# Output pairs of a two-layer encoder: one weight sum moved from an accumulating DMA to VectorE, and residual and memory loads spread over the last pair

## The chip, the cores and the metric

The kernel runs on one core of one Trainium2 chip. The metric is device time in microseconds (us). Before the change it is 1529.16 us, the median of three runs (1528.39 to 1529.31). TensorE is called PE in the profile, VectorE DVE, ScalarE ACT, GpSimd POOL and SyncE SP.

## The reference

An encoder of two layers over 512 positions of width 2048, in float32. Of one layer (cut):

```python
h = rmsnorm(x, pre_norm_g[l])
z = h @ w_in[l]                    # 2048 x 4928, split into latents, conv, memory query, gate
a_out = mla_attention(q, k, v)     # 8 heads, 512 positions
c_out = short_gated_conv(gb, gc, xin, conv_w[l])
m_out = memory_attention(q_mem, rmsnorm(mem, mem_norm_g[l]), w_mk[l], w_mv[l])
y = jnp.concatenate([a_out, c_out, m_out], axis=-1) * jax.nn.silu(gate)
o = y @ w_o[l]                     # 2048 x 2048
x = x + rmsnorm(o, post_norm_g[l])
```

The change is about the last two lines: the output projection, and the residual sum behind its norm.

## The kernel before, in words

**Products in two halves.** Every float32 operand is split into a high half (fp32r) and the rest, and each product is three matmuls (`mm3`, lines 245, 246, 247: high by high, high by low, low by high). `prep` splits a weight block of 128x1024: ScalarE casts the block `wr` into `wh` (line 172), VectorE subtracts to get `wl` (line 173). For the memory's weights a gain is multiplied in, in two halves of 512 columns (lines 177 and 178).

**Seven products for eight.** A projection is computed by pairs of 512 output columns in the Strassen-Winograd form: the weight's four blocks B11, B12, B21, B22 and four sums of them, the left operand's blocks and sums, and seven products P1 to P7. One product is four steps (c = 0 to 3), each with one weight block of 128x1024, 512 KB. `unit` says where a step's weight operand comes from. In the output pairs P1 uses B11, loaded by SP into a tile T, which has a buffer of its own for each c. P5 uses T after B12 was added to it (this sum is T1), P6 after B22 was added, P4 after B21 was added. P2 uses B21 by itself, P3 uses B22, and P7 uses B22 after B12 was added. Each of these additions is an **accumulating DMA** that POOL issues (`more`, line 134, `accum_op=ALU.add`): it is issued as soon as both halves of the block's previous use are split. So one output pair has 16 of them: four each for P5, P6, P4 and P7.

**The order of the work.** The output projection of a layer has two pairs, g0 (the first) and g1 (the last). Each goes through the passes P2, P1, P5, P6 and P3 in turn, P7, P4; P2 of g0, and of g1, is put elsewhere. `Program.run` walks over the steps. Before each it has SP load weight blocks (`load`, a ring of RAW = 8 buffers, in which T keeps its own while it is in use) and prepares (`prep`) blocks two steps ahead. Evictions, gains and norms are put off (`defer`) and taken from a list as each step's `room` allows. PE, SP and POOL run in the order in which the program is written; the order on DVE and ACT is set by a scheduler at build time. The order also fixes each queue: an engine waits for its next instruction's operands even where a later one could run.

**Behind the last pair.** `fetch(t)` is a DMA on POOL that loads 128 rows of the residual x (or, in layer 1, of the scratch `xs`), 1 MB, into a tile `xr` (line 1125). `mem_reload(h)` loads one half of the turned memory, two tiles mH and mL of 1 MB each, from the scratch `mTd`, on POOL (line 671). When a row tile's four column blocks are done, `factor` reduces its squares (`tot`, DVE, line 1148), POOL computes the factor r (`ms` line 255, `r` line 257), and DVE adds the scaled output to xr in two halves (line 1155); POOL writes the new rows to `xs` (line 1159), or SP the output in layer 1. Products are evicted on DVE by lines 430, 457 and 460 and on ACT by line 465; line 1110 squares and line 1115 multiplies by the gain on DVE. In layer 1 P4 of the last pair holds its four weight blocks at once in tiles T4h and T4l (`hold`). The memory's products (mk, mv) of the next layer start right behind P4 of layer 0, with the mH and mL of `mem_reload(0)`.

Of the kernel before, what the change touches and what calls it, by code (L numbers as in the profile page):

```python
# [5 lines left out]
F32 = mybir.dt.float32  # L6
# [3 lines left out]
ALU = mybir.AluOpType  # L10
AX = mybir.AxisListType

P = 128
# [3 lines left out]
NT = S // P  # L17
# [46 lines left out]
class Unit:  # L64
# [2 lines left out]

    def __init__(self, key, loads=(), more=None, alloc=None, gain=None):  # L70
        self.key = key
        self.loads = loads
        self.more = more
        self.alloc = alloc
        self.gain = gain


class Program:
# [19 lines left out]
    def add(self, fn, units=(), room=0.0, ahead=None):  # L98

        self.steps.append((list(units), fn, room, self.ahead if ahead is None else ahead))  # L100
# [14 lines left out]
    def run(self):  # L115
        nc = self.nc
        raw, hip, lop = self.pools
        seq = [u for us, *_ in self.steps for u in us]
        tiles, outs = {}, {}
        at = {"load": 0, "prep": 0}  # L120
        users = {}
        for c, u in enumerate(seq):
            users.setdefault(u.key, []).append(c)
        after = {a: b for cs in users.values() for a, b in zip(cs, cs[1:])}
        first_more = [c for c, u in enumerate(seq) if u.more is not None and users[u.key][0] == c]

        def move(engine, t, off, src, **kw):
            n = 1
            for d in src.shape[1:]:
                n *= d  # L130
            dst = t[:, off:off + n]
            if len(src.shape) == 3:
                dst = dst.rearrange("p (a b) -> p a b", b=src.shape[2])
            engine.dma_start(dst, src, **kw)  # L134
            return off + n

        def load(upto):
            upto = max(upto, self.early)
            while at["load"] < min(upto, len(seq)):
                u = seq[at["load"]]  # L140
                if u.loads:
                    t = raw.tile([P, 1024], F32, tag="raw", name=f"wr{len(tiles)}")
                    off = 0
                    for src in u.loads:
                        off = move(nc.sync, t, off, src)
                    tiles[u.key] = t[:, :off]
                at["load"] += 1

        def more(c):
            u = seq[c]  # L150
            move(nc.gpsimd, tiles[u.key], 0, u.more, accum_op=ALU.add)

        self.load = load

        def prep(upto):
            while at["prep"] < min(upto, len(seq)):
                c = at["prep"]
                load(c + 1)
                while first_more and first_more[0] <= c + self.more_ahead:
                    load(first_more[0] + 1)  # L160
                    more(first_more.pop(0))
                u = seq[c]
                src = tiles[u.key]
                at["prep"] += 1
                n = src.shape[-1]
                if u.alloc is None:
                    hi = hip.tile([P, 1024], F32R, tag="wh", name=f"wh{c}")
                    lo = lop.tile([P, 1024], F32R, tag="wl", name=f"wl{c}")
                else:
                    hi, lo = u.alloc()  # L170
                if u.gain is None:
                    nc.scalar.copy(hi[:, :n], src)  # L172
                    nc.vector.tensor_tensor(lo[:, :n], src, hi[:, :n].bitcast(F32), op=ALU.subtract)  # L173
                else:
                    for k, g in enumerate(u.gain()):
                        h = slice(k * (n // 2), (k + 1) * (n // 2))
                        nc.scalar.activation(hi[:, h], src[:, h], AF.Copy, scale=g)  # L177
                        nc.vector.scalar_tensor_tensor(lo[:, h], src[:, h], g, hi[:, h].bitcast(F32),  # L178
                                                       op0=ALU.mult, op1=ALU.subtract)
                outs[c] = (hi[:, :n], lo[:, :n])  # L180
                if c in after:
                    more(after[c])

        self.prep = prep
        c = 0
        spare = 0.0
        for units, fn, room, ahead in self.steps:
            n = len(units)
            if n:
                load(c + n + self.ahead + self.loads_ahead)  # L190
                prep(c + n + ahead)
            fn(*[outs.pop(c + i) for i in range(n)])
            c += n
            spare = min(spare + room, 2.5)
            while self.queue and spare >= self.queue[0][0]:
                cost, put_off = self.queue.pop(0)
                spare -= cost
                put_off()


def encoder(tc, x, mem, positions, pre_norm_g, w_in, q_norm_g, w_uq, kv_norm_g, w_ukv, conv_w,
# [3 lines left out]
    nc = tc.nc  # L205
# [18 lines left out]
    G = {}  # L224
# [180 lines left out]
    STEADY = [["P1"], ["P5", "P2"], ["P6", "P3"], ["P7"], ["P4"]]  # L405
    SECOND = [["P2"], ["P1"], ["P5"], ["P6", "P3"], ["P7"], ["P4"]]

    def group(left, key, w, block, slot, passes, final, hold=None, by_two=False):

# [5 lines left out]

        def unit(q, c):
            def of(name, *loads, more=None, alloc=None):
                return Unit((key, name, c), [block(h, j, c) for h, j in loads],  # L420
                            None if more is None else block(*more, c), alloc)
            if q == "P1":
                return of("P1" if apart else "T", (0, 0))
            if q == "P5":
                return of("T", *([(0, 0)] if apart else []), more=(0, 1))
            return {"P6": lambda: of("T", more=(1, 1)), "P4": lambda: of("T", more=(1, 0), alloc=hold),
                    "P2": lambda: of("P2", (1, 0)), "P3": lambda: of("B22", (1, 1)),
                    "P7": lambda: of("B22", more=(0, 1))}[q]()
# [84 lines left out]

        def room(q, c):
            if c < 3:
                return 1.4
            moves = {"P1": passes is SECOND, "P2": passes is not SECOND, "P5": apart, "P7": 1 + apart}
            return 1.4 - 1.4 * moves.get(q, 1)

# [555 lines left out]
    def out_proj(l):  # L1075
# [17 lines left out]
        def block(g):  # L1093
            def f(h, j, c):
                r = h * 1024 + c * 256
                k = (2 * g + j) * 512
                return w_o[l, r:r + 256, k:k + 512].rearrange("(a p) c -> p a c", p=P)
            return f

        def slot(g):  # L1100
            return lambda i, j, tt: og(2 * i + tt)[:, (2 * g + j) * 512:(2 * g + j + 1) * 512]
# [32 lines left out]
            hold_n[0] += 1  # L1134
            return tuple(t[:, k * 1024:(k + 1) * 1024] for t in st["hold"])

        g0 = group(G["left"], ("o", l, 0), 512, block(0), slot(0), SECOND, fin(0))
        g1 = group(G["left"], ("o", l, 1), 512, block(1), slot(1), SECOND, fin(1), hold if last else None)
        return g0, g1, gains, fetch

    def residual(l, st, t):
# [40 lines left out]
    def put(*passes):  # L1182
        for steps in passes:
            for s in steps:
                add(*s)
# [26 lines left out]
    for l in range(depth):  # L1212
# [7 lines left out]
        if l == 0:  # L1220
            add(use)
            def turn_half(t, h, on=None):
                return lambda: transpose_rows(0, t, G[f"hs{t}"], (2 * h, 2 * h + 1), on)
            add(turn_half(0, 0))
            add(lambda: first_rows(1, (0,)))
            add(pr.begin_prep(1))
            add(lambda: left_half(0, (0,)))
            add(pr.begin_prep(2))
            add(turn_half(1, 0, nc.scalar))
            add(lambda: first_rows(1, (1,)))  # L1230
            add(lambda: left_half(1, (0,)))
            add(pr.begin_prep(3))
            add(lambda: first_factor(2))
            add(turn_half(0, 1))
        else:
            ms = mem_steps(l)
            put(ms[:1])
            add(use)
            for n in range(16):
                t, q = n // 4, n % 4  # L1240
                if q == 0:
                    add(lambda t=t: pr.until(lambda: f"hs{t}" in G))
                add(lambda t=t, q=q: transpose_rows(l, t, G[f"hs{t}"], (q,)))
                if t < 2 and q % 2:
                    add(lambda t=t, q=q: left_half(t, (q // 2,)))
                if t >= 2 and q == 3:
                    add(lambda t=t: right_half(t - 2))
                put(ms[n + 1:n + 2])
        (a, b), (a1, b1) = gs[0][:2], gs[1][:2]
        add(owns[0])  # L1250
        if l == 0:
# [77 lines left out]
                G["src"], G["dst"] = x[0], dram.tile([S, D], F32, name="xs")  # L1329
        add(route)  # L1330
        add(gains(1))
        put(*g1[1:3])
        put(g1[3])
        for t in range(NT):
            add(fetch(t))
        if l + 1 < depth:
            add(lambda: mem_reload(0))
        put(g1[4])
        if l + 1 < depth:
            add(lambda: mem_reload(1))  # L1340
        put(g1[5])
        if l + 1 == depth:
            add(pr.settle)

# [26 lines left out]
```

## Time and profile before

| what | value |
|---|---|
| median of three runs | 1529.16 us |
| profiled execution, its own time | 1529.26 us |
| span of the profiled execution | 1527.5 us |
| granted TensorE clock, mean | 0.994 |
| PE busy | 1493.4 us (98%) |
| DVE busy | 1040.1 us (68%) |
| DMA of POOL's queue | 141.57 MB, 48.5% of 16 engines' span |
| DMA of SP's queue | 132.68 MB, 26.7% of 16 engines' span |

A row of a timeline reads: start in us, time in us, engine, line, operation, output and inputs, count, and in brackets the idle time of the engine just before and what ended it. A row of the chain of work reads: start, time, what held the end at that moment. In layer 0 the last pair's P5 runs from 705.6 us, P6 and P3 from 716.5, P7 from 738.4, P4 from 749.1; in layer 1 the same stages come some 750 us later.

### The profile page before, as it was taken

Reading aid. Unit: us, or ns where it says so; the run is one execution under the profiler, and the core shown is the slowest. Engines: PE = TensorE matmul, PEld = TensorE weight load, DVE = VectorE, ACT = ScalarE, POOL = GpSimd, SP = SyncE. Lnnn points to the kernel's source line nnn. Section 1 sums busy time; section 2 is a strip of 40 time slices with the busy share of each in tenths; the row PEclk is TensorE's granted clock in tenths of the full one; section 3 lists DMA queues with packets and bytes.
Section 4 is the critical chain, followed back from the end, with each engine's and each line's share of the span. In section 5 each row is a group of like instructions: output and inputs, shape, how many; then the busy total and the mean of one; then the engine's idle time right before and its main releaser. Section 6 shows DMA issues by size and latency. Waiting matters only on the chain.

```text
span 1527.5 us, 20239 instructions
## 1 busy us (share of the span) xinstructions
PE 1493.4 (98%) x7613; PEld 1281.3 (84%) x7613; DVE 1040.1 (68%) x1398; ACT 864.7 (57%) x1335; POOL 314.9 (21%) x313
## 2 busy tenths in 40 slices
PE   9999999999999999999999999999999999999996
PEld 7888888988898888888788888888988888888884
DVE  6965675565968668865778766675566586687656
ACT  7733534454768768645578434434454686775542
POOL 1233131332000000324320333131332000003231
PEclk9999999999999999999999999999999999999998
DMA  8999898989581112699997999897989411048895
GB/s 330 216 213 224 204 174 174 199 196 256 164 264 56 42 42 82 109 202 197 313 332 239 238 224 226 187 176 168 198 207 222 130 59 39 29 111 146 203 200 222
DMA packets 146934, 275.59 MB, mean 180 GB/s; under 512 B 17340, under 2 KB 40212, under 8 KB 143508
## 3 DMA queue, kind: packets, MB, share of 16 engines
q0 software_dynamic: 65600, 141.57, 48.5%
q1 hardware_dynamic: 81104, 132.68, 26.7%
q8 instruction: 59, 0.97, 0.3%
q14 instruction: 39, 0.32, 0.1%
q10 hardware_dynamic: 132, 0.05, 0.0%
HBM read 259.59 MB, written 14.68 MB: 180 GB/s over the span
## 4 chain that ended last, share of the span: by engine, by line
PE 85%; DVE 4%; DMA 3%; issue 3%; ACT 3%; POOL 2%; POOLq 0%; DVEq 0%; ACTq 0%
PE P L246 20%; PE P L247 20%; PE P L245 19%; PE ptp L973 2%; PE tps L731 1%; DMA mL<-mTd 1%; PE o L246 1%; PE sc L245 1%; PE mk L246 1%; PE sc L246 1%; PE sc L247 1%; PE mk L247 1%; PE o L247 1%; PE o L245 1%; DVE wl L173 1%
## 5 line engine op out<-in xcount | busy, mean ns | idle before, releaser
L173 DVE TENSOR_TENSOR wl<-wr,wh 128x1024 fp32r<-128x1024 f32 (+1 forms) x408 | 486.4, 1196 | 334.6 <-ACT wh L172 332.2
L172 ACT CAST wh<-wr 128x1024 fp32r<-128x1024 f32 (+1 forms) x408 | 420.6, 1033 | 482.5 <-PE P L247 418.2
L246 PE MATMUL P<-wl,S 128*128 128x512 f32 (+1 forms) x896 | 344.2, 384 | 2.8 <-DVE wl L173 2.8
L245 PE MATMUL P<-wh,S 128*128 128x512 f32 (+1 forms) x896 | 346.0, 386 | 0.0
L247 PE MATMUL P<-wh,S 128*128 128x512 f32 (+1 forms) x896 | 343.4, 383 | 0.0
L134 POOL DMA_DIRECT2D wr<-in_w_in_dram x160 | 193.4, 1209 | 484.5 <-DVE wl L173 365.2
L246 PE MATMUL P<-wl,A 128*128 128x512 f32 (+1 forms) x656 | 251.9, 384 | 2.1 <-DVE wl L173 2.1
L245 PE MATMUL P<-wh,A 128*128 128x512 f32 (+1 forms) x656 | 253.1, 386 | 0.2 <-ACT wh L172 0.2
L247 PE MATMUL P<-wh,A 128*128 128x512 f32 (+1 forms) x656 | 251.6, 384 | 0.5 <-DVE A L251 0.5
L246 PEld LDWEIGHTS P<-wl,S 128*128 128x128 f32 x896 | 168.3, 188 | 33.7 <-DVE wl L173 4.4
L247 PEld LDWEIGHTS P<-wh,S 128*128 128x128 f32 x896 | 168.2, 188 | 30.4
L245 PEld LDWEIGHTS P<-wh,S 128*128 128x128 f32 x896 | 168.1, 188 | 29.6 <-ACT wh L172 0.2
L134 POOL DMA_DIRECT2D wr<-in_w_o_dram x64 | 77.3, 1208 | 505.0 <-DVE rec L961 352.0
L246 PEld LDWEIGHTS P<-wl,A 128*128 128x128 f32 x656 | 123.2, 188 | 24.4 <-DVE wl L173 2.9
L247 PEld LDWEIGHTS P<-wh,A 128*128 128x128 f32 x656 | 123.1, 188 | 23.3 <-DVE A L251 1.2
L245 PEld LDWEIGHTS P<-wh,A 128*128 128x128 f32 x656 | 123.1, 188 | 22.3 <-ACT wh L172 0.6
L959 ACT ACTIVATE P<-sc,nm 128x512 f32<-128x512 f32 (+1 forms) x96 | 59.9, 624 | 36.4 <-DVE nm L956 35.8
L962 ACT ACTIVATE P<-P,rec 128x512 f32<-128x512 f32 (+1 forms) x96 | 62.1, 658 | 5.0 <-DVE rec L961 5.0
L956 DVE TENSOR_REDUCE nm<-sc 128x1 f32<-128x512 f32 (+1 forms) x96 | 57.2, 596 | 10.0 <-PE sc L954 6.3
L251 DVE TENSOR_TENSOR PT<-ptp,PT 128x512 fp32r<-128x512 f32 (+1 forms) x96 | 56.5, 594 | 8.5 <-ACT PT L250 8.1
L178 DVE SCALAR_TENSOR_TENSOR wl<-wr,cols,wh 128x512 fp32r<-128x512 f32 x64 | 46.2, 747 | 18.2 <-ACT wh L177 18.0
L177 ACT ACTIVATE wh<-wr,cols 128x512 fp32r<-128x512 f32 x64 | 44.2, 722 | 25.2 <-PE mk L246 10.9
(267 smaller groups left out, 2182.4 us busy)
## 6 DMA issues: line engine op xcount, KB each, us to landing
wr<-in_w_in_dram POOLq DMA_DIRECT2D x128, 512.0 KB, 6.9
wr<-in_w_in_dram SPq DMA_DIRECT2D x112, 512.0 KB, 5.6
wr<-in_w_o_dram POOLq DMA_DIRECT2D x64, 512.0 KB, 7.3
wr<-in_w_o_dram SPq DMA_DIRECT2D x48, 512.0 KB, 3.9
wr<-in_w_in_dram POOLq DMA_DIRECT2D x32, 416.0 KB, 5.4
wr<-in_w_in_dram SPq DMA_DIRECT2D x24, 416.0 KB, 4.3
wr<-in_w_mk_dram SPq DMA_DIRECT2D x16, 512.0 KB, 6.9
wr<-in_w_mv_dram SPq DMA_DIRECT2D x16, 512.0 KB, 4.5
```

The costliest lines, as they stand in the source:

```text
L134: engine.dma_start(dst, src, **kw)
L172: nc.scalar.copy(hi[:, :n], src)
L173: nc.vector.tensor_tensor(lo[:, :n], src, hi[:, :n].bitcast(F32), op=ALU.subtract)
L177: nc.scalar.activation(hi[:, h], src[:, h], AF.Copy, scale=g)
L178: nc.vector.scalar_tensor_tensor(lo[:, h], src[:, h], g, hi[:, h].bitcast(F32), op0=ALU.mult, op1=ALU.subtract)
L245: nc.tensor.matmul(ps, ah, bh, start=first, stop=False, **kw)
L246: nc.tensor.matmul(ps, ah, bl, start=False, stop=False, **kw)
L247: nc.tensor.matmul(ps, al, bh, start=False, stop=last, **kw)
L251: nc.vector.tensor_tensor(lo, src, hi.bitcast(F32), op=ALU.subtract)
L956: nc.vector.tensor_reduce(nmax, ps, axis=AX.X, op=ALU.max, negate=True)
L959: nc.scalar.activation(pt, ps, AF.Exp, bias=nmax, accum_out=tot)
L962: nc.scalar.activation(pt, pt, AF.Copy, scale=rec)
```

## The change

Two things are changed. First, in both output pairs T1 is summed by VectorE: B12 is loaded by SP into a raw buffer of its own (`plus`), and `prep` adds it to T ahead of P5's split. The accumulating DMA of P5 is not issued, and the room of P5's first three steps goes from 1.4 to 0.2. The other accumulations (P6, P4, P7) stay. Second, the four residual loads and the memory's reloads are issued at other steps of the last pair.

```diff
                     for src in u.loads:
                         off = move(nc.sync, t, off, src)
                     tiles[u.key] = t[:, :off]
+                if u.plus is not None:
+                    t = raw.tile([P, 1024], F32, tag="raw", name=f"wr{len(tiles)}")
+                    off = move(nc.sync, t, 0, u.plus)
+                    tiles[at["load"]] = t[:, :off]
                 at["load"] += 1
...
                 src = tiles[u.key]
+                if u.plus is not None:
+                    nc.vector.tensor_tensor(src, src, tiles[c], op=ALU.add)
...
-                if c in after:
+                if c in after and seq[after[c]].more is not None:
                     more(after[c])
...
+                loads = [block(h, j, c) for h, j in loads]
+                more = None if more is None else block(*more, c)
+                if q in by_vector:
+                    return Unit((key, name, c), loads, plus=more, alloc=alloc)
+                return Unit((key, name, c), loads, more, alloc=alloc)
...
             if c < 3:
-                return 1.4
+                return 0.2 if q in by_vector else 1.4
...
-        g0 = group(G["left"], ("o", l, 0), 512, block(0), slot(0), SECOND, fin(0))
-        g1 = group(G["left"], ("o", l, 1), 512, block(1), slot(1), SECOND, fin(1), hold if last else None)
+        g0 = group(G["left"], ("o", l, 0), 512, block(0), slot(0), SECOND, fin(0), by_vector=("P5",))
+        g1 = group(G["left"], ("o", l, 1), 512, block(1), slot(1), SECOND, fin(1), hold if last else None,
+                   by_vector=("P5",))
...
                 put(ms[n + 1:n + 2])
+                if n == 0:
+                    add(lambda: mem_reload(1))
...
-        put(*g1[1:3])
-        put(g1[3])
-        for t in range(NT):
-            add(fetch(t))
+        put(g1[1], g1[2][:1])
+        add(fetch(0))
+        put(g1[2][1:], g1[3][:1])
+        add(fetch(1))
+        put(g1[3][1:4])
+        add(fetch(2))
+        put(g1[3][4:])
         if l + 1 < depth:
             add(lambda: mem_reload(0))
-        put(g1[4])
-        if l + 1 < depth:
-            add(lambda: mem_reload(1))
-        put(g1[5])
+        put(g1[4][:2])
+        add(fetch(3))
+        put(g1[4][2:], g1[5])
```

PE's order of matmuls is the same. POOL's queue in layer 0, at the end of the last pair, before (`wr<-in_w_o_dram` is an accumulating DMA of 512 KB, `xr` a residual load of 1 MB, `mH` and `mL` the memory):

```order
L134 DMA wr_6208<-in_w_o_dram 128x2x512
L134 DMA wr_6446<-in_w_o_dram 128x2x512
L255 TENSOR_SCALAR ms_6613<-tot_637_6611 128x1
L257 TENSOR_TENSOR r_6615<-ms_6613,mhalf 128x1
L1125 DMA xr_6617<-in_x_dram 128x2048
L1125 DMA xr_6619<-in_x_dram 128x2048
L1125 DMA xr_6621<-in_x_dram 128x2048
L1125 DMA xr_6623<-in_x_dram 128x2048
L671 DMA mH_6625<-mTd 128x2048
L671 DMA mL_6626<-mTd 128x2048
L1159 DMA xs<-xr_6617 128x1024 x2
```

And now, from the second residual load on:

```order
L1136 DMA xr_6502<-in_x_dram 128x2048
L135 DMA wr_6379<-in_w_o_dram 128x2x512
L135 DMA wr_6198<-in_w_o_dram 128x2x512
L135 DMA wr_6427<-in_w_o_dram 128x2x512
L1136 DMA xr_6557<-in_x_dram 128x2048
L135 DMA wr_6216<-in_w_o_dram 128x2x512
L135 DMA wr_6464<-in_w_o_dram 128x2x512
L262 TENSOR_SCALAR ms_6635<-tot_640_6633 128x1
L264 TENSOR_TENSOR r_6637<-ms_6635,mhalf 128x1
L682 DMA mH_6639<-mTd 128x2048
L682 DMA mL_6640<-mTd 128x2048
L1171 DMA xs<-xr_6425 128x1024 x2
```

Three residual loads (the first stands three accumulations ahead of these rows' start) are now among the accumulations, the last of which, wr_6464, is the sum of B22 for P7's last step; mH and mL stand right behind the first r. The fourth residual load stands behind the second r, the second memory reload behind the third pair of writes to xs.

VectorE in the second pair, at P1 and P5 in layer 0, where the additions are; before (wr_5484 and wr_5539 are P4's blocks of the first pair, wr_6152 and the following ones T of the second):

```order
L173 TENSOR_TENSOR wl_6235<-wr_5484,wh_6234 128x1024
L1115 TENSOR_TENSOR og_5553<-og_5553,g_616_5834 128x512
L1115 TENSOR_TENSOR og_5564<-og_5564,g_616_5834 128x512
L173 TENSOR_TENSOR wl_6251<-wr_5539,wh_6250 128x1024
L173 TENSOR_TENSOR wl_6267<-wr_6152,wh_6266 128x1024
L173 TENSOR_TENSOR wl_6284<-wr_6172,wh_6283 128x1024
L430 TENSOR_TENSOR og_5553<-og_5553,P_617_5841 128x512
L430 TENSOR_TENSOR og_5564<-og_5564,P_618_5842 128x512
L173 TENSOR_TENSOR wl_6312<-wr_6190,wh_6311 128x1024
```

And now:

```order
L180 TENSOR_TENSOR wl_6263<-wr_5539,wh_6262 128x1024
L180 TENSOR_TENSOR wl_6281<-wr_6160,wh_6280 128x1024
L170 TENSOR_TENSOR wr_6160<-wr_6160,wr_6242 128x1024
L180 TENSOR_TENSOR wl_6299<-wr_6180,wh_6298 128x1024
L441 TENSOR_TENSOR og_5553<-og_5553,P_617_5846 128x512
L441 TENSOR_TENSOR og_5564<-og_5564,P_618_5847 128x512
L170 TENSOR_TENSOR wr_6180<-wr_6180,wr_6260 128x1024
L1126 TENSOR_TENSOR og_5553<-og_5553,g_615_5838 128x512
L1126 TENSOR_TENSOR og_5564<-og_5564,g_615_5838 128x512
L180 TENSOR_TENSOR wl_6326<-wr_6198,wh_6325 128x1024
```

Line 170 is the new addition; it stands behind the split of P1's block of the same T. In the first pair three of its four stand among the last attention work, ahead of the stage that starts at 639 us.

VectorE in layer 1, from P7's last split on, before:

```order
L1148 TENSOR_REDUCE tot_1260_13084<-ssqo_1191_12026 128x1
L1148 TENSOR_REDUCE tot_1271_13142<-ssqo_1195_12037 128x1
L173 TENSOR_TENSOR wl_13119<-wr_12919,wh_13118 128x1024
L1155 SCALAR_TENSOR_TENSOR xr_13090<-og_12025,r_13088,xr_13090 128x1024 x2
L460 SCALAR_TENSOR_TENSOR og_12027<-P_1267_13102,og_12027 128x512
L460 SCALAR_TENSOR_TENSOR og_12038<-P_1268_13103,og_12038 128x512
L1115 TENSOR_TENSOR og_12027<-og_12027,g_1253_12782 128x512
L173 TENSOR_TENSOR T4l_13123<-wr_12626,T4h_13122 128x1024
L173 TENSOR_TENSOR T4l_13123<-wr_12646,T4h_13122 128x1024
```

And now (T4l of the first two blocks stands in one row each, the second of them eleven rows above these, ahead of P3's last split):

```order
L1160 TENSOR_REDUCE tot_1263_13122<-ssqo_1191_12042 128x1
L1160 TENSOR_REDUCE tot_1270_13172<-ssqo_1195_12053 128x1
L1167 SCALAR_TENSOR_TENSOR xr_12914<-og_12041,r_13126,xr_12914 128x1024
L180 TENSOR_TENSOR wl_13149<-wr_12953,wh_13148 128x1024
L1167 SCALAR_TENSOR_TENSOR xr_12914<-og_12041,r_13126,xr_12914 128x1024
L180 TENSOR_TENSOR T4l_13181<-wr_12688,T4h_13180 128x1024
L1167 SCALAR_TENSOR_TENSOR xr_12991<-og_12052,r_13176,xr_12991 128x1024 x2
```

The T4 splits of the first two blocks moved ahead of the residual; one half of the residual now stands ahead of P7's last split (wl_13149), in layer 0 as in layer 1.

More of the change, by code (lines that the diff above doesn't have):

```diff
@@ L64, with __init__ @@
 class Unit:
-    def __init__(self, key, loads=(), more=None, alloc=None, gain=None):
+    def __init__(self, key, loads=(), more=None, plus=None, alloc=None, gain=None):
         self.key = key
@@ L73, in __init__ @@
         self.more = more
+        self.plus = plus
         self.alloc = alloc
@@ L406, in encoder, with group @@
     SECOND = [["P2"], ["P1"], ["P5"], ["P6", "P3"], ["P7"], ["P4"]]
-    def group(left, key, w, block, slot, passes, final, hold=None, by_two=False):
+    def group(left, key, w, block, slot, passes, final, hold=None, by_two=False, by_vector=()):
         bk = {}
@@ L419, in of @@
             def of(name, *loads, more=None, alloc=None):
-                return Unit((key, name, c), [block(h, j, c) for h, j in loads],
-                            None if more is None else block(*more, c), alloc)
+                loads = [block(h, j, c) for h, j in loads]
[3 more added lines that the diff above has]
+                return Unit((key, name, c), loads, more, alloc=alloc)
             if q == "P1":
```

## The prediction

> **What bounds the kernel now.** I read the page first, then the list of waits of TensorE, then the chain of work and the timelines around the three longest waits.
>
> ```profile
> span 1527.5 us, 20239 instructions
> PE 1493.4 (98%) x7613; PEld 1281.3 (84%) x7613; DVE 1040.1 (68%) x1398; ACT 864.7 (57%) x1335; POOL 314.9 (21%) x313
> PE P L246 <- DVE wl L173: 5.0, 5, 1.4
> PE P L245 <- ACT T4h L172: 4.7, 1, 4.7
> PE mk L246 <- DMA mL<-mTd: 3.2, 1, 3.2
> PE mk L247 <- DVE wl L178: 1.3, 1, 1.3
> ```
>
> TensorE is busy 98% of the span, so only two things can be won: its waits, and the time in which it runs at a lower rate behind a wait. The list of waits has the columns waiting engine and line, releaser, total us, times, longest. Three of its rows belong to this change: the 4.7 on T4h, the 3.2 on mL and parts of the first. Here is how the one on mL arises, at the end of layer 0.
>
> ```profile
> 742.36 1.47 POOL r L257
> 743.82 2.71 DMA xr<-in_x_dram
> 746.53 19.35 DMA mL<-mTd
> 749.88 2.48 DVE L1155 SCALAR_TENSOR_TENSOR xr<-og,r,xr 128x1024 f32<-128x1024 f32 x2 [3.72 <-DMA xr<-in_x_dram]
> 751.81 0.39 PE L245 MATMUL P<-wh,A 128*128 128x512 f32 x1
> 753.55 0.50 PE L246 MATMUL P<-wl,A 128*128 128x512 f32 x1 [1.36 <-DVE wl L173]
> 762.34 0.36 PE L245 MATMUL mk<-mH,wh 128*128 128x256 f32 x1 [0.54 <-DMA mH<-mTd]
> 766.50 0.21 PE mk L247
> 770.98 0.21 PE mk L247
> 784.06 0.12 PE mk L245
> ```
>
> POOL starts the four residual loads only behind r, at 743.82, and the memory loads behind them. VectorE waits 3.72 for the first residual load, with the splits of P4 queued behind it, so TensorE waits 1.36 at 753.55. mL takes 19.35 from its issue at 746.53, to 765.88, because six transfers of 1 MB lie in a row: TensorE waits 0.54 and then 3.2. After that its matmuls start 0.21 apart for 24 of them (766 to 771), where at 784 the same matmul takes 0.12: 24 x 0.09 = 2.2 more. This place costs 0.54 + 3.2 + 2.2 = **5.9**, and the one on VectorE **1.36**.
>
> The end of layer 1 is the other place:
>
> ```profile
> 1492.88 5.13 DMA xr<-xs
> 1498.12 2.48 DVE xr L1155 x2
> 1502.92 0.95 ACT T4h L172
> 1503.91 0.80 PE L245 MATMUL P<-T4h,A 128*128 128x512 f32 x1 [4.71 <-ACT T4h L172]
> 1505.17 0.80 PE L246 MATMUL P<-T4l,A 128*128 128x512 f32 x1 [0.46 <-DVE T4l L173]
> 1506.19 0.63 PE L245 MATMUL P<-T4h,A 128*128 128x512 f32 x1
> 1508.75 0.43 PE L245 MATMUL P<-T4h,A 128*128 128x512 f32 x1
> 1509.02 0.40 PE L246 MATMUL P<-T4l,A 128*128 128x512 f32 x1
> 681.66 0.23 PE P L247
> ```
>
> The residual load is issued at 1492.88, VectorE stands until 1498.12, and what is queued behind it (the eviction of P7, then the squares and T4h on ScalarE) ends in a wait of 4.71. Between 1503.91 and 1509.02 TensorE starts ten matmuls in 5.11; at its usual 0.23 apart (as at 681.66) they take 2.3. So this place costs 4.71 + 2.8 = **7.5**. The Trainium skill ("TensorE: Matmul & The Clock Gate", Part 1: The HAM clock gate) says that an idle window of about 3.4 us drops the clock to a half until some 3.4 us of work have gone by; the trace agrees: spacing 0.43 behind the wait of 4.71, 0.21 against 0.12 behind one of 3.2, and nothing of the kind behind 1.36.
>
> A smaller place lies in the first pair of layer 0:
>
> ```profile
> 669.04 9.69 DMA wr<-in_w_o_dram
> 681.16 0.50 PE L246 MATMUL P<-wl,S 128*128 128x512 f32 x1 [0.76 <-DVE wl L173]
> ```
>
> An accumulating DMA lands 9.69 after its issue, since others lie ahead of it: **0.76**.
>
> **The change part by part.** *The sum by VectorE.* It takes 16 accumulating DMAs off POOL's queue (4 for each of 2 pairs in 2 layers) and adds 16 plain loads by SP and 16 additions of 128x1024.
>
> ```profile
> L173 DVE TENSOR_TENSOR wl<-wr,wh 128x1024 fp32r<-128x1024 f32 (+1 forms) x408 | 486.4, 1196 | 334.6 <-ACT wh L172 332.2
> 639.20:650.00 10.80, 10.80 (x49) 8.96 (x48) 10.80 (x12) 8.08 (x11) 5.83 (x5) 1.00 0.94 159
> 705.50:716.40 10.90, 10.90 (x50) 9.03 (x49) 7.16 (x8) 6.15 (x9) 4.77 (x4) 1.00 1.13 207
> 749.10:761.80 12.70, 11.34 (x49) 8.73 (x47) 11.44 (x14) 8.77 (x14) 3.72 (x6) 1.00 1.03 417
> ```
>
> The L173 row is the same kind of instruction on the same shape at 1.196, so the additions are 16 x 1.2 = 19.1 of VectorE's time. In the second pair VectorE is busy 7.16 of 10.9 in the stage of P5 (the columns of the windows are PE, PEld, DVE, ACT, POOL, clock, DMA share, GB/s), so four additions of 4.8 come to 12.0 for that stage and its neighbours; the evictions, which the plan puts off while P5 runs (room 0.2 for 1.4), go to later stages. In the first pair the stage from 639.2 is full (10.80 of 10.80), but by VectorE's order three of the four additions stand before it. Nothing uncovered is the one bound, one addition of 1.2 in each layer the other; nearest are the half-idle stages, so I take 0.3 in all (0 to 2.4). SP's 16 loads come before each pair's queue on POOL is busy; I take 0 for them and keep their price for a rival.
>
> *What goes.* The wait at 681.16 (0.76): the four accumulations ahead of it are gone. The 1.36 at 753.55, the 5.9 at mL (both residual data and memory are now asked for earlier; mH and mL stand directly behind r), the 7.5 at T4h (the first two T4 splits are now ahead of the residual). Of the 1.3 on the memory's split, mk L247 (queued behind a residual that waits for r) I take half, 0.7, since that wait for r stays (0 to 1.3). Sum: 0.76 + 1.36 + 5.9 + 7.5 + 0.7 = **16.2**.
>
> *What comes.* Three residual loads of 1 MB now lie in POOL's queue among the second pair's 12 accumulations, ahead of the last two, and TensorE needs the last one, the sum of B22 for P7's last step.
>
> ```profile
> 701.41 1.23 DVE L173 TENSOR_TENSOR wl<-wr,wh 128x1024 fp32r<-128x1024 f32 x1 [1.50 <-ACT wh L172]
> 704.13 1.23 DVE L173 TENSOR_TENSOR wl<-wr,wh 128x1024 fp32r<-128x1024 f32 x1 [1.50 <-ACT wh L172]
> 707.06 1.19 POOL L134 DMA_DIRECT2D wr<-in_w_o_dram  x1 [2.83 <-DMA wr<-in_w_o_dram]
> 720.11 1.21 POOL L134 DMA_DIRECT2D wr<-in_w_o_dram  x1 [1.14 <-DVE wl L173]
> 730.28 1.21 POOL L134 DMA_DIRECT2D wr<-in_w_o_dram  x1 [1.35 <-DVE wl L173]
> 732.97 1.21 POOL L134 DMA_DIRECT2D wr<-in_w_o_dram  x1 [1.47 <-DVE wl L173]
> wr<-in_w_o_dram POOLq DMA_DIRECT2D x64, 512.0 KB, 7.3
> 1491.49 1.05 ACT L172 CAST wh<-wr 128x1024 fp32r<-128x1024 f32 x1 [0.69 <-DMA wr<-in_w_o_dram]
> ```
>
> When due: a step takes 2.72 (701.41 to 704.13). P4's second step starts at 751.81, so P7's last starts two steps earlier, at 746.4, and 0.23 later needs the low half of its split, behind 1.05 on ScalarE and 1.23 on VectorE: the sum must land by 744.2 (with 0.1 for hand-offs). In layer 1 P7 ends 4.71 before 1503.91, at 1499.2; its last step starts at 1496.5 and the sum is due at 1494.2. When it lands: before, at 732.97 + 7.3 = 740.3 in layer 0 and at 1491.45 in layer 1. The queue serves one accumulation in (730.28 - 720.11) / 4 = 2.54. One residual load costs it between 2.5 (1 MB at the 417 GB/s of the stage from 749.1) and 5.1 (1492.88, alone); I take 2.9, near the lower end, since the 5.1 holds a latency that is hidden in a queue. Three: +8.7. Against that the queue starts earlier: P6's first accumulation was issued at 707.06 only because the queue was full; its split is done at 701.41 + 1.23 = 702.6, so up to 4.4 earlier; I take 3.5, since the first come one per step and not one per 2.54. Memory weights that SP loads beside the last ones (layer 0 only): +1.5. So the last sum lands at 740.3 + 8.7 - 3.5 + 1.5 = 747.0, **2.8 late**, in layer 0, and at 1491.45 + 5.2 = 1496.65, **2.4 late**, in layer 1. Bounds: 0 late on the one side (4.4 earlier and 2.5 each); on the other the queue starts no earlier and each is 2.9, 6.3 and 6.0 late. Waits of 1.36 show no slow stretch and one of 3.2 does (2.2), so I take 0 for it, up to 2 in each layer.
>
> *P4 in layer 0.* Behind the late sum VectorE has five splits, three residual halves (2.48 for two) and four evictions and products (1.28 for two), in the order that it has after the change.
>
> ```profile
> 753.41 1.28 DVE L460 SCALAR_TENSOR_TENSOR og<-P,og 128x512 f32<-128x512 f32 x2
> ```
>
> That is 6.1 + 3.7 + 2.6 = 12.4. It has from 747.0 + 1.05 = 748.05 until P4's last step needs its low half, 751.81 + 2 x 2.72 + 2.8 + 0.23 = 760.3: 12.2. I take 0.5 with hand-offs (0 to 2). Sum of what comes: 2.8 + 2.4 + 0.5 + 0.3 = **6.0**.
>
> **The sum**: -16.2 + 6.0 = -10.2, made against the profiled execution, 1529.26 (span 1527.5 and 1.8 around it), which stands 0.1 above the median 1529.16. So 1519.1.
>
> **Rivals.** (A) *The last sum is in time*: the queue's early start and faster residual loads hide it. For it: between 701 and 707 nothing is then in the queue. Against: from 705.5 the share of the DMA engines is 1.13 already. -16.2 + 0.8 = -15.4, 1513.9. (B) *VectorE is late in the first pair*: the full stage from 639.2 pushes splits behind the additions, 2 to 5 a layer, 1523 to 1529. Against: the evictions that fill that stage can be put off, and the additions stand before it. (C) *Slower: the residual loads hold the queue.* Place: the last sum for P7 in both layers. Price: if each of the three takes 5.13, as alone, the sum is 6.7 later than I have it, 9.5 and 9.1 late, with a slow stretch of 2 behind each: 22.6 + 0.8 - 16.2 = +7.2, 1536. It decides from about 7 late in each layer on, that is from some 4.5 for each load. For it: the queue is served in order, and its DMA share is full; against: six such transfers with SP's loads beside them took 765.88 - 743.82 = 22.1, 3.7 each. The Trainium skill ("DMA: Bandwidth & Descriptors", Issuing engines are not separate DMA queues) says that transfers started by different engines share the same 16 engines; that speaks against moving blocks from POOL to SP. In this trace plain transfers move 417 GB/s at a share of 1.03 and accumulating ones 207 at 1.13, so a moved block still asks for half its engine time; by the rule, were they to fall into the busy stretch, four of them would delay the last sum by about 5.
>
> **How the numbers follow.** My forecast (waits of some 1 to 5 in P7, the rest gone) 0.58; A 0.15; B 0.13, half of which ends within 0.2%; C 0.14. A change under 0.2% (3.1 us) can't be told from none. Faster 0.58 + 0.15 + 0.05 = 0.78, same 0.08 (B's end, 1526 to 1532), slower 0.14. The range takes A's end (1512.5: all 16.2 and the other half of the mk wait gone, nothing comes) and the bounds of the late sums: 12.3 of lateness, 2 on VectorE and a slow stretch of 2 end at 1529.4. C lies outside.
>
> **What would show it.** Right: no wait of TensorE on T4h or on mL, no slow matmuls at 766; a new wait of 1 to 5 on the split of P7's last step (near 746 and 1496), whose releaser is an accumulating DMA; 16 additions of 1.2 with no wait of TensorE at P5. Wrong: a wait of over 5 there with matmuls 0.43 apart behind it (C), waits at P5 or P6 near 640 to 660 (B), or none at all (A).

## The result, and the profile after

The changed kernel takes 1527.79 us (median of 21 runs, 1525.93 to 1530.4), the kernel before 1529.56 us in the same comparison (21 runs). The ratio is 0.9987, with a 95% interval of 0.9981 to 0.9994: some 1.8 to 2 us faster, where 10.2 were forecast. The profiled execution took 1526.53 us, with a span of 1524.8.

The page of the changed kernel:

```profile
span 1524.8 us, 20252 instructions
PE 1491.6 (98%) x7613; PEld 1279.5 (84%) x7613; DVE 1058.0 (69%) x1414; ACT 863.7 (57%) x1335; POOL 296.2 (19%) x297
```

Its list of TensorE's waits (waiting engine and line, releaser, total us, times, longest):

```profile
PE P L252 <- ACT wh L179: 10.0, 3, 7.0
PE P L253 <- DVE wl L180: 4.0, 5, 1.0
```

The waits on T4h, on mL and on the memory's split are gone from the list, as the forecast had it. What is new is a row of 10.0 on the cast of a weight block, with one wait of 7.0 in it. The timeline of TensorE and the chain of work show where it comes from. First the chain at P7's last step, in layer 0 and then in layer 1:

```profile
736.87 14.16 DMA wr<-in_w_o_dram
751.12 1.05 ACT wh L179
...
1487.85 9.80 DMA wr<-in_w_o_dram
1497.72 1.05 ACT wh L179
```

And TensorE's timeline at these places:

```profile
752.21 0.80 PE L252 MATMUL P<-wh,S 128*128 128x512 f32 x1 [6.97 <-ACT wh L179]
753.47 0.80 PE L253 MATMUL P<-wl,S 128*128 128x512 f32 x1 [0.46 <-DVE wl L180]
...
1498.82 0.50 PE L252 MATMUL P<-wh,S 128*128 128x512 f32 x1 [2.84 <-ACT wh L179]
1500.08 0.80 PE L253 MATMUL P<-wl,S 128*128 128x512 f32 x1 [0.76 <-DVE wl L180]
```

The last accumulating DMA, the sum of B22 for P7's last step, lands at 736.87 + 14.16 = 751.0 in layer 0 (before: 740.8; forecast 747.0; due 744.2) and at 1487.85 + 9.80 = 1497.6 in layer 1 (before: 1491.4; forecast 1496.65; due 1494.2). TensorE waits 7.4 and 3.6 for it, in two pieces each, the high half and then the low half of the split.

Behind these waits it also runs slowly. In the windows view the columns are PE, PEld, DVE, ACT, POOL, granted clock, DMA share, GB/s:

```profile
753.50:756.00 2.50, 2.50 (x6) 2.02 (x7) 2.25 (x2) 1.29 (x1) 0.53 (x1) 0.50 1.02 401
1500.00:1502.00 2.00, 1.92 (x5) 1.53 (x6) 2.00 (x3) 0.66 (x1) 0.00 (x0) 0.50 0.91 381
```

And two matmuls of the first stretch in the timeline:

```profile
754.49 0.63 PE L252 MATMUL P<-wh,S 128*128 128x512 f32 x1
754.92 0.63 PE L253 MATMUL P<-wl,S 128*128 128x512 f32 x1
```

The granted clock is 0.50 in both stretches, and the matmuls start 0.43 apart, against a usual 0.23. So the slow stretches of before have not gone; they moved to P7.

### The profile page after: what moved, and what is told of

Same layout as the page of the kernel before. It is cut to its first block, busy times and chain, and to the rows that moved or that the text cites. A ratio compares the mean times of both kernels' runs of the same rounds, so it can differ in the third digit from the quotient of the medians.

```text
span 1524.8 us, 20252 instructions
## 1 busy us (share of the span) xinstructions
PE 1491.6 (98%) x7613; PEld 1279.5 (84%) x7613; DVE 1058.0 (69%) x1414; ACT 863.7 (57%) x1335; POOL 296.2 (19%) x297
## 4 chain that ended last, share of the span: by engine, by line
PE 91%; DVE 3%; ACT 3%; DMA 2%; issue 1%; POOL 1%; DVEq 0%; POOLq 0%; ACTq 0%
PE P L253 22%; PE P L254 22%; PE P L252 22%; PE ptp L984 2%; DMA wr<-in_w_o_dram 2%; PE tps L742 1%; PE o L253 1%; PE sc L252 1%; PE sc L253 1%; PE sc L254 1%; PE o L254 1%; PE o L252 1%; PE mk L253 1%; PE mk L254 1%; PE mk L252 1%; PE sc L964 1%
## 5 line engine op out<-in xcount | busy, mean ns | idle before, releaser
L135 POOL DMA_DIRECT2D wr<-in_w_o_dram x48 | 57.8, 1203 | 166.1 <-DVE wl L180 146.7
L1100 POOL DMA_DIRECT2D g<-in_post_norm_g_dram x8 | 5.5, 813 | 368.7 <-PE ptp L984 368.6
```

## The experiments

Ten kernels were run. The theory: the change's gains are real, and the residual loads that now stand among the accumulations give most of them back, since they make the last B22 sum late (the queue theory). The first rival: the additions by VectorE, with their loads, are the cause (the addition theory). Later ones: it is the memory weights that SP loads beside the queue; it is POOL's queue and not the transfer.

| kernel | median us | ratio to before, 95% interval |
|---|---|---|
| changed kernel | 1527.79 | 0.9987 (0.9981 to 0.9994) |
| vector_sum_only | 1529.77 | 0.9999 (0.9990 to 1.0008) |
| spread_loads_only | 1527.12 | 0.9983 (0.9974 to 0.9992) |
| memory_weights_held | 1527.85 | 0.9987 (0.9978 to 0.9996) |
| memory_weights_by_pool | 1524.94 | 0.9972 (0.9961 to 0.9982) |
| two_residuals_early | 1522.78 | 0.9959 (0.9946 to 0.9971) |
| one_residual_early | 1513.57 | 0.9893 (0.9879 to 0.9906) |
| none_early | 1513.09 | 0.9895 (0.9882 to 0.9909) |
| one_early_dma_sum | 1514.42 | 0.9899 (0.9884 to 0.9914) |
| none_early_dma_sum | 1513.14 | 0.9905 (0.9887 to 0.9923) |
| residuals_by_sp | 1527.4 | 0.9989 (0.9980 to 0.9998) |

### Each half by itself

vector_sum_only puts the residual loads back behind the last pair, and the memory's reloads to their old places (shortened):

```diff
-        put(g1[1], g1[2][:1])
-        add(fetch(0))
...
+        put(*g1[1:3])
+        put(g1[3])
+        for t in range(NT):
+            add(fetch(t))
```

Expected:

> Only the first half of the change: the sum T1 by VectorE, with the residual and memory loads behind the last pair as before. Queue theory (the residual loads among the accumulations make the last B22 sum late, the addition is harmless): no wait of TensorE on P7's last step in either layer, the waits of 4.7 on T4h and 3.2 on mL are still there, the 0.76 in the first pair is gone; 1527 to 1529.5 us. Addition theory (the additions and their SP loads push the queue late from its start): a wait of 2 or more at P7's last step, and over 1530 us.

Measured: 1529.77, the time of before. Its waits:

```profile
PE P L252 <- ACT T4h L179: 4.7, 1, 4.7
PE mk L253 <- DMA mL<-mTd: 3.5, 1, 3.5
```

Both old waits are there and none at P7. The additions cost nothing that can be measured in the time, and bring nothing either. The waits are those of the queue theory, the time is 0.3 above its range; the addition theory asked for a wait at P7 and over 1530, and falls. The last sum is not quite untouched: in layer 0 it lands 9.7 after its issue at 733.66, at 743.4, and 2.6 later than before (740.8), which is still in time.

spread_loads_only takes the sum back:

```diff
-        g0 = group(..., SECOND, fin(0), by_vector=("P5",))
+        g0 = group(..., SECOND, fin(0))
```

(and the same for g1). Expected:

> Only the second half: loads spread over the last pair, T1 still summed by accumulating DMAs. Queue theory: 16 accumulations and three residual loads in one queue, so the last B22 sum lands still later than in the changed kernel (about 751 and 1498), at 752 to 756 and 1499 to 1503; waits of 7 to 11 and 4 to 8 at P7's last step; 1529 to 1535 us, no gain over before. Addition theory: the waits at P7 shrink below the 7.0 and 2.8 of the changed kernel, 1519 to 1524 us.

Measured: 1527.12, the time of the changed kernel, and the chain has the last sum at

```profile
737.60 13.87 DMA wr<-in_w_o_dram
1488.39 9.79 DMA wr<-in_w_o_dram
```

that is at 751.5 and 1498.2, only 0.4 and 0.5 later than with the sum by VectorE, and the time is below the 1529 expected. So the queue theory was wrong in one point: four accumulations fewer hardly bring the last one forward. The change's small gain is that of the loads.

### How many residual loads stand ahead of the last sum

one_residual_early, two_residuals_early and none_early differ from the changed kernel in the places of the loads alone. The edit of one_residual_early:

```diff
         put(g1[1], g1[2][:1])
         add(fetch(0))
-        put(g1[2][1:], g1[3][:1])
+        put(g1[2][1:], g1[3][:7])
         add(fetch(1))
-        put(g1[3][1:4])
-        add(fetch(2))
-        put(g1[3][4:])
+        put(g1[3][7:])
         if l + 1 < depth:
             add(lambda: mem_reload(0))
-        put(g1[4][:2])
+        put(g1[4][:1])
+        add(fetch(2))
+        put(g1[4][1:2])
         add(fetch(3))
         put(g1[4][2:], g1[5])
```

In two_residuals_early the first two loads stay where the change put them, the third comes behind `g1[3][:7]`, and the fourth stays. In none_early the first comes behind `g1[3][:7]`, the second behind the memory reload, the third and fourth as here. Expected:

> The changed kernel with only the first residual load among the accumulations; the second stands right behind the last accumulation, the other two in P4. Queue theory: two loads of 1 MB fewer ahead of the last B22 sum, 5.5 us earlier, at 743 to 745.5 and 1491.5 to 1492.5; TensorE's wait there falls from 7.0 and 2.8 to 0 to 1.5 and 0; no wait on T4h or mL of over 1; 1515 to 1520 us. Addition theory: the waits at P7 stay over 4 and 2; 1525 us or more.

> The changed kernel with two residual loads among the accumulations (three in the changed kernel, one in one_residual_early); the third stands right behind the last accumulation. Queue theory: each residual load ahead of the last sum costs 2.4 to 2.8: it lands at 746 to 748.5 and at 1494.5 to 1495.5; waits of 2 to 4.5 and of 0.3 to 1.5, with or without the slow stretch; 1515.5 to 1521 us, between the two kernels. If only the third load or its place matters: 1513 to 1515 us.

> No residual load among the accumulations: the first stands right behind the last accumulation, ahead of r, the second behind the memory reload, the others in P4. Queue theory: the last sum lands at 738 to 741.5 and at 1489 to 1490 and makes nobody wait; but the first residual load lands 5 to 6 behind it, at 744 to 747 and 1494.5 to 1496, while r is there at 743 and 1493, so VectorE waits 1 to 4 and TensorE 0 to 3 in P4; 1512 to 1518 us. If a residual load has to be early for the gain: 1522 us or more.

Measured: 1513.57, 1522.78 and 1513.09. The last accumulation of none_early in layer 0, its issue and its time to landing:

```profile
731.84 1.21 POOL L135 DMA_DIRECT2D wr<-in_w_o_dram  x1 [1.38 <-DVE wl L180]
```

```profile
wr<-in_w_o_dram POOLq DMA_DIRECT2D x1, 512.0 KB, 8.2
```

P7's last step in layer 0, the chain and then the timeline, of one_residual_early:

```profile
734.03 9.51 DMA wr<-in_w_o_dram
```

```profile
745.97 0.50 PE L253 MATMUL P<-wl,S 128*128 128x512 f32 x1 [0.65 <-DVE wl L180]
```

and of two_residuals_early:

```profile
737.06 10.75 DMA wr<-in_w_o_dram
```

```profile
748.98 0.79 PE L252 MATMUL P<-wh,S 128*128 128x512 f32 x1 [3.61 <-ACT wh L179]
750.24 0.80 PE L253 MATMUL P<-wl,S 128*128 128x512 f32 x1 [0.47 <-DVE wl L180]
```

With none, one, two and three residual loads ahead the last sum lands at 740.0, 743.5, 747.8 and 751.0 in layer 0, and TensorE waits 0.48, 0.65, 4.1 and 7.4 for the split. So the first load is covered by the slack and costs 0.5 in the whole, less than the runs can tell; the second costs 9.2 and the third 5.0.

The second costs more than its waits, since it brings a slow stretch in both layers. In layer 1 of two_residuals_early the sum is late by little, but behind two short waits the matmuls start 0.42 to 0.43 apart, from 1495.06 to 1498.05:

```profile
1492.97 0.50 PE L252 MATMUL P<-wh,S 128*128 128x512 f32 x1 [0.86 <-ACT wh L179]
1494.23 0.51 PE L253 MATMUL P<-wl,S 128*128 128x512 f32 x1 [0.76 <-DVE wl L180]
...
1495.49 0.63 PE L254 MATMUL P<-wh,S 128*128 128x512 f32 x1
1495.91 0.63 PE L252 MATMUL P<-wh,S 128*128 128x512 f32 x1
```

Two runs missed their ranges: one_residual_early came out below (1515 to 1520), and two_residuals_early above (1515.5 to 1521), with waits at or just over the upper ends (4.1 of 4.5, 1.6 of 1.5) and both slow stretches. In none_early VectorE waits 2.70 for the first residual load, within the 1 to 4 expected; TensorE waits the 0.48.

### The memory weights beside the queue

memory_weights_held kept `load` from issuing mk and mv blocks until two steps of P7 were written:

```diff
+                if self.held and u.key[0] in ("mk", "mv"):
+                    break
```

> The changed kernel with SP's loads of the next layer's memory weights held back until two steps of P4 are through, so that none lies beside the last accumulations. If these plain loads cost the queue 4 us at the end of layer 0: the last B22 sum lands at 746 to 748 there, the wait of 7.0 becomes 2 to 4 and the slow stretch behind it goes; layer 1 is unchanged (2.8); 1521 to 1524 us. If the residual loads alone make it late: the wait stays at 6 or more and the time within 1 us of 1527.8.

Measured: 1527.85, and SP issues the first of them when it did before, at 734.26 (733.76 in the changed kernel). Writing them later in the program did not hold them back; I take it that nothing else stands between them in SP's order. The run says nothing on the question. (The expectation names steps of P4; the steps are P7's.)

memory_weights_by_pool gives the first three to POOL, written behind the memory reload (shortened; the lines that hold them until there are as above):

```diff
+                by = nc.gpsimd if u.key in (("mk", 1, 0), ("mv", 1, 0), ("mk", 1, 1)) else nc.sync
...
-                        off = move(nc.sync, t, off, src)
+                        off = move(by, t, off, src)
```

> The changed kernel with the next layer's first three memory weight loads issued by POOL behind the memory reload, so that no plain load of SP lies beside the last accumulations of layer 0. If these loads cost the queue 3 to 4 us there: the last B22 sum lands at 747 to 748.5 (now 751.0), TensorE's wait of 7.0 becomes 3 to 4.5, layer 1 stays at 2.8; 1521 to 1525 us. If the residual loads alone make it late: 751 and the wait of 7 stay, 1527 to 1528.5 us.

The chain and the timeline in layer 0:

```profile
736.66 10.63 DMA wr<-in_w_o_dram
```

```profile
748.47 0.51 PE L256 MATMUL P<-wh,S 128*128 128x512 f32 x1 [3.48 <-ACT wh L183]
```

Measured: 1524.94; the last sum lands at 747.3 in layer 0, 3.7 earlier than in the changed kernel, and the waits for it fall from 7.4 to 4.2. So the plain loads beside the queue cost it 3.7 there, as expected.

### Queue or transfer, and the sum once more

residuals_by_sp:

```diff
-                nc.gpsimd.dma_start(st["x"][t], G["src"][t * P:(t + 1) * P, :])
+                (nc.sync if t < 3 else nc.gpsimd).dma_start(st["x"][t], G["src"][t * P:(t + 1) * P, :])
```

> The changed kernel with its three early residual loads issued by SP instead of POOL, at the same steps, so that they don't stand in the queue of the accumulations. If the place in POOL's queue is what delays the last B22 sum: it lands at 740 to 744 and 1489 to 1492, no wait of over 1 at P7's last step, 1513 to 1517 us. If it is the transfer itself, whichever queue it comes from (the DMA engines are shared): the sum still lands 4 to 7 later than without them, waits of 3 to 7 and 1.5 to 3.5 stay, 1521 to 1528 us.

The chain in layer 0 and in layer 1, and the timeline of both:

```profile
736.70 11.41 DMA wr<-in_w_o_dram
...
1467.02 7.31 DMA wr<-in_w_o_dram
1474.35 1.05 ACT T4h L179
```

```profile
749.28 0.80 PE L252 MATMUL P<-wh,S 128*128 128x512 f32 x1 [3.73 <-ACT wh L179]
1476.39 0.79 PE L252 MATMUL P<-wh,S 128*128 128x512 f32 x1 [4.46 <-ACT wh L179]
```

Measured: 1527.4. In layer 0 the last sum lands at 748.1, 3 earlier than from POOL's queue, but still 8.1 later than with no residual load early (740.0), a little more than the 4 to 7 expected. In layer 1 the wait moved ahead, to 1476.4, behind the split of a T4 block whose accumulation landed only at 1474.3. So the transfer counts wherever it is issued, and its place in POOL's queue is not the cause by itself. This is what the Trainium skill says ("DMA: Bandwidth & Descriptors", Issuing engines are not separate DMA queues): the engines that start transfers share the same DMA engines. The run agrees. It does not say how much of the 3 is the queue and how much the earlier start, since SP issued the loads earlier than POOL (all three by 704, POOL at 707.7, 722.0 and 729.7).

one_early_dma_sum and none_early_dma_sum are one_residual_early and none_early with `by_vector` taken out of both groups, as in spread_loads_only; the second is the kernel before with another order of loads and nothing else.

> The kernel one_residual_early (1513.6 us), but with T1 summed by accumulating DMAs as before. If the sum by VectorE hardly brings the queue forward (P6's first accumulation is issued when its split is done, not when the queue has room), the last B22 sum lands 0 to 1 later, the 0.4 to 0.8 of the first pair come back, and it takes 1513.5 to 1516 us. If four accumulations of 2.5 fewer are what makes room, the last sum lands 5 to 10 later, TensorE waits 3 to 8 in each layer, and it takes 1520 us or more.

> The kernel before with only its loads put in the order of none_early (1513.1 us): T1 summed by accumulating DMAs. If the sum by VectorE is worth nothing here: 1513 to 1515 us. If it is worth the 2.5 us for each accumulation that it takes off the queue: a wait of 1 or more at P7's last step in either layer and 1516 us or more.

Measured: 1514.42 and 1513.14, beside 1513.57 and 1513.09 with the sum by VectorE. The sum is worth nothing here that can be told from none. Nor does it bring the last sum forward: counted in layer 0 from the issue of P6's first accumulation, the last one lands 0 to 2.1 later with the sum by VectorE than without it, in each of the four pairs of kernels. P6's first accumulation shows where the early start went. In none_early, with the sum by VectorE, the row of POOL's timeline and the row of its time to landing (the last column) are

```profile
701.63 1.23 POOL L135 DMA_DIRECT2D wr<-in_w_o_dram  x1 [33.00 <-DVE wl L180]
```

```profile
wr<-in_w_o_dram POOLq DMA_DIRECT2D x1, 512.0 KB, 9.3
```

and in none_early_dma_sum

```profile
701.31 1.18 POOL L135 DMA_DIRECT2D wr<-in_w_o_dram  x1 [1.50 <-DVE wl L180]
```

```profile
wr<-in_w_o_dram POOLq DMA_DIRECT2D x1, 512.0 KB, 8.5
```

POOL had been idle for 33 us with the one and was in the middle of its stream with the other, but the accumulation is issued at the same time, when the split that it waits for is done; and it lands no earlier. Beside it, from 700.05 on, SP loads two weight blocks that the other kernel had issued by 688; that they are what slows it is argued from this one pair.

Each of none_early, one_residual_early and their versions without VectorE's sum is 15 to 16 us faster than the kernel before in the same comparison, and 13 to 15 faster than the changed kernel.

## Why the prediction was wrong, point by point

**What goes: right in sum, in part by luck.** Forecast 16.2. The kernel nearly without the new waits, none_early, is 1529.45 - 1513.09 = 16.4 faster than the kernel before on its chip. By layers, from the last attention matmul that waits in one layer to the same in the next, and from there to the end of the span; before, after and none_early:

```profile
626.88 0.39 PE L246 MATMUL o<-PT,V 128*128 128x256 f32 x1 [0.70 <-DVE PT L251]
1377.62 0.39 PE L246 MATMUL o<-PT,V 128*128 128x256 f32 x1 [0.70 <-DVE PT L251]
```

```profile
626.42 0.39 PE L253 MATMUL o<-PT,V 128*128 128x256 f32 x1 [0.70 <-DVE PT L258]
1377.41 0.39 PE L253 MATMUL o<-PT,V 128*128 128x256 f32 x1 [0.70 <-DVE PT L258]
```

```profile
span 1511.1 us, 20243 instructions
```

```profile
626.53 0.39 PE L253 MATMUL o<-PT,V 128*128 128x256 f32 x1 [0.69 <-DVE PT L258]
1367.08 0.39 PE L253 MATMUL o<-PT,V 128*128 128x256 f32 x1 [0.69 <-DVE PT L258]
```

| stretch, us | before | changed | none_early |
|---|---|---|---|
| layer 0's to layer 1's | 750.74 | 750.99 | 740.55 |
| layer 1's to the end | 149.9 | 147.4 | 144.0 |

So 10.2 and 5.9 were to be had, where my terms by layer come to 8.7 and 7.5: two misses that nearly cancel. In layer 0 all of the 1.3 on the memory's split went, of which I took half; the other 0.9 I can't place. In layer 1 none_early pays for waits of 0.63 and 0.67 on T4l of its own. The changed kernel gave back 10.4 and 3.4: **13.8, where I had 6.0**. 16.1 - 13.8 = 2.3 is what is left in the profiled executions (2.7 by their spans, with 0.5 of it ahead of these stretches).

**What comes: wrong, and this is the step that failed.** The mechanism was named (the last sum late, TensorE waiting on P7's last step); the step that failed is the sum of how late that sum comes and what the lateness costs. Three of its terms erred the same way: the credit for the queue's early start was too large, the memory weights and the slow stretch were too small.

*The queue's early start, 3.5.* This was a misread row. I took the accumulation at 707.06 as P6's first, held up by a full queue. It is the second; the first was issued at 703.05. P6's first accumulation before, in layer 0, its issue in POOL's timeline and its time to landing:

```profile
703.05 1.18 POOL L134 DMA_DIRECT2D wr<-in_w_o_dram  x1 [1.51 <-DVE wl L173]
```

```profile
wr<-in_w_o_dram POOLq DMA_DIRECT2D x1, 512.0 KB, 8.8
```

and after in layer 0:

```profile
701.51 1.23 POOL L135 DMA_DIRECT2D wr<-in_w_o_dram  x1 [33.00 <-DVE wl L180]
```

```profile
wr<-in_w_o_dram POOLq DMA_DIRECT2D x1, 512.0 KB, 9.6
```

It landed at 711.85 before and at 711.1 after: 0.7 earlier, not 3.5. In both kernels its issue waits for the split (the releaser is wl), so an empty queue could not bring it forward; and after, it took 9.6 instead of 8.8, with SP's loads beside it.

*The three residual loads, 8.7: a little high.* In layer 1, where no memory weights are loaded, the last sum came 6.2 later; with a start that is at most 1 earlier, the three loads cost some 7, 2.4 each (2.9 forecast).

*Memory weights beside the queue, 1.5: too low.* In layer 0 the last sum came 10.3 later: 0.7 earlier at the start, 7 for the residual loads, and 3.7 to 4 for the plain loads, which memory_weights_by_pool took away (3.7). Before, the queue ended at 740.8, and the first of them, issued at 735.31, landed 6.3 later, at 741.6. After, the last two accumulations are issued behind the first of them (733.76), at 734.34 and 736.87, and take 12.8 and 14.2, where the last two of layer 1, without such loads, take 9.8 each. Held up by the residual loads, the queue ran into them.

*The slow stretch, 0 forecast, up to 2 as its bound: too low.* In layer 0 the waits are 7.4 and the loss 10.4. At the clock of 0.50 every matmul is 0.43 behind the last for 0.23, and the stretch lies on P7's and P4's matmuls. In layer 1 too the clock was 0.50, behind waits of 2.84 and 0.76: the eight matmuls from 1498.82 to 1503.12 take 4.3, of which 0.76 is the wait and 1.8 their usual time. So a late sum costs its wait and about 3 more in layer 0 and 1.7 more in layer 1. That only 3.4 is lost there in the whole is in part because the changed kernel lacks none_early's 1.3 on T4l. The ground for the 0 was wrong too: a single wait of 1.36 shows no slow stretch, but the two of 0.86 and 0.76 in two_residuals_early do, so a wait of 3.2 is not needed for one. The idle window of about 3.4, for which the prediction cites the Trainium skill, did not occur there either; the measurement decides.

Put together, the last sum came 6.8 late in layer 0 and 3.4 late in layer 1 (forecast 2.8 and 2.4). In layer 0 the 4.0 between them are, about, 2.8 of early start that was not there, some 2.3 of memory weights and 0.5 by which the sum of before landed later than the 740.3 that I reckoned, less 1.7 for the residual loads. By its place, and by the sign that I gave for it (a wait of over 5 with matmuls 0.43 apart), layer 0 is rival C, at a smaller price and not for C's reason: a residual load did not cost more than I had it; the queue started later and ran into SP's loads. A time within 0.2% of before had a chance of 0.08, and for another cause, VectorE in the first pair (B), of which the runs show nothing.

**The additions by VectorE: right** (0.3 forecast). Line 170 in the changed kernel, durations in ns, first and last start:

```profile
L170 DVE TENSOR_TENSOR wr<-wr,wr x16: 1214/1218/1225, 614.5 to 1452.0; 128x1024 f32<-128x1024 f32 x16
```

Each takes 1.2, and no wait for any of the 16 shows. **The 0.76 of the first pair** is gone in the changed kernel and in vector_sum_only, and too small to show in the whole of vector_sum_only. **P4 in layer 0, 0.5:** TensorE waits for no split of P4 in the changed kernel. It may be that the late sum hid it; no run shows that.

What stays open: how much of a residual load's price is order in the queue and how much sharing of the engines, why P6's first accumulation takes 9.6 beside SP's loads, and 0.9 of the gain in layer 0.

## What to carry to other kernels

Before a transfer is spread into a stretch because its engine is idle there, look for the last transfer of the stream that it is put into, and when that one is due: here three loads, each asked for 30 us and more ahead of its use, pushed a sum past its due time that had some 3 us to spare. Put such loads right behind the last urgent transfer, which here was worth 14 us more than the spread; putting the first of them early as well gained nothing on top (1513.57 against 1513.09). And to find what sets a transfer's issue, name the row exactly (the first or the second of its kind) before an advance is reckoned from it.

## What the runs showed of the hardware

An accumulating DMA took longer beside plain loads even with nothing ahead of it: 9.6 to landing for P6's first accumulation in the changed kernel, with POOL idle for 33 us before it and two SP loads beside. That is more than the 5.8 of the one at 642.90 in the same kernel, with SP's nearest load issued 7 earlier, and more than the 7.4 that is the median of all these accumulations there:

```profile
wr<-in_w_o_dram POOLq DMA_DIRECT2D x48, 512.0 KB, 7.4
```

Residual loads issued by SP delayed the last accumulation too: 748.1 against 740.0 with none early, where POOL's made it 751.0.

Two waits of 0.86 and 0.76 with one matmul between them were enough for a granted clock of 0.50 (two_residuals_early, 1495 to 1497), as were 2.84 and 0.76 in the changed kernel; a wait of 1.36 by itself, before, had left it at 1.00.
